# Hybrid decoder trunk on one core: modulation steps behind every second mixing unit, join masks on ScalarE, one form of the 16-block inverses through DRAM

## The chip, the cores and the metric

One Trainium2 chip, one of its cores. The metric is the device time of one execution in microseconds; before the change it is 1177.0 us (median of three runs, 1176.92 to 1178.7). The engines are named as in the profile: PE is TensorE (PEld its weight loads), DVE is VectorE, ACT is ScalarE, POOL is GpSimd, SP the engine that issues most DMAs.

## The reference, cut to what matters

Two layers; in each a half-step SwiGLU FFN, a token-mixing sub-layer and a second FFN, all on 256 tokens of width 1024, each modulated by shift, scale and gate vectors made from `c`. A 64x64 unit-triangular system is inverted for every head and chunk of the mixing's third head group.

```python
def reference(x, c, ...):
    c_act = jax.nn.silu(c)
    for l in range(DEPTH):                                   # 2 layers
        mod = c_act @ w_ada[l] + b_ada[l]                    # 1024 x 9216 matrix: nine vectors
        sh1, sc1, gt1, sh2, sc2, gt2, sh3, sc3, gt3 = jnp.split(mod, N_MOD, axis=-1)
        h = modulate(x, ln_ffn1_g[l], sh1, sc1)
        x = x + 0.5 * gt1[:, None, :] * swiglu(h, ffn1_w_gate[l], ffn1_w_up[l], ffn1_w_down[l])
        h = modulate(x, ln_mix_g[l], sh2, sc2)
        x = x + gt2[:, None, :] * token_mixing(h, w_in[l], ...)
        h = modulate(x, ln_ffn2_g[l], sh3, sc3)
        x = x + 0.5 * gt3[:, None, :] * swiglu(h, ffn2_w_gate[l], ffn2_w_up[l], ffn2_w_down[l])
    return rmsnorm(x, final_g)

def gated_delta_net(q, k, v, g, beta):                       # 6 heads, chunks of 64
    ...
    L = jnp.where(strict, jnp.einsum('bhncd,bhnsd->bhncs', k_beta, k) * decay, 0.0)
    T = lax.linalg.triangular_solve(eye + L, jnp.broadcast_to(eye, L.shape), left_side=True, lower=True)
    u = T @ v_beta
```

## The kernel before

All weights stay in float32 in DRAM and stream through four 1 MB tiles of SBUF (`raw`, N_RAW = 4). A piece of weights is a granule (`gran`); its transfer is issued on SP's queue as soon as the tile that it takes is released. Most granules are then converted into a high and a low part, `hi` by ScalarE and `lo` by VectorE (`convert`), at most six units ahead of their use (N_UNIT), and each product is three matmuls. The units named in WHOLE (`gqk`, `cg`, `ca`, `gv`) are read by PE straight from the raw tile, which is released when PE is done with it.

The nine modulation vectors of a layer are matrix-vector products. A vector needs four modulation steps (`adaunit` in the plan, `ada_step` when it runs): one 1 MB granule of `w_ada`, and two VectorE operations that multiply its rows by a column of `c_act` and add them to an accumulator (`adaacc` or `Lb`). Then `extract` has PE transpose the accumulator in two halves of four transposes into the bank `px`, VectorE reduces each half, and `complete` adds bias and gain. `need_mod` runs all that is still missing at the place where the vector is wanted; `begin_next` wants the next sub-layer's scale and shift (6 and 7 behind the mixing) before the last two output units of the mixing run.

The sequence in which units are converted is written by `plan_ffn` and `plan_mix`. In the mixing, the function `unit` (L344) counts the converted units (six of `mqk`, four of `mv`, three of `gz`) and puts a modulation step behind the second of them and then behind every fourth; what is left in `todo` comes behind the eight units of the output projection. Layer 0 has eight such steps (vectors 6 and 7), layer 1 has four (vector 7).

The order of each engine's queue is written out by hand-made rules at build time: `Clock` keeps a planned time for every engine (`cost`, `note`), PE works through the units, and at `tick` the side tasks of the mixing (generators that `yield` what they wait for) put in their pieces when the planned clock says that their inputs are ready. The engines then run these queues in order. The planned clock counts nothing for the time in which GpSimd issues its DMAs.

The side tasks that matter here: `decays` makes the decay exponents: VectorE spreads `g` over two tiles (`spread`), PE adds them up, and a small matmul gives `cross`. `pairs` forms the matrices L in LD (buffer `xin_LT`) and sends their 32-blocks to DRAM (`scr_l`). `inverse` reads the 16-blocks from there into `Lb`, and GpSimd inverts them by 15 steps of two short operations, a product into `T` and a subtraction from `W`. The inverses are written in both forms (plain and transposed) to `scr_w`, at their places in zeroed 32-blocks, and read back as `Wc`; PE joins them with the off-diagonal blocks `Um` (LD times a mask, GpSimd) to inverses of 32, and then of 64. `values_beta` transposes `v` by PE; `delta_rule` uses inverses and values. `taps` runs the 31-tap convolution on VectorE, or on ScalarE (product, `ctap`) and GpSimd (sum, `cacc`).

Of the kernel before, what the change touches and what calls it, by code (L numbers as in the profile page):

```python
# [10 lines left out]
F32 = mybir.dt.float32  # L11
# [35 lines left out]
CA = dict(b_ada=0, ln_ffn1_g=72, ln_mix_g=96, ln_ffn2_g=104, conv_b=112, conv_ln_g=114, conv_ln_b=116, gdn_norm_g=118)  # L47
CA_PARTS = (slice(0, 80), slice(96, 119))
CB = dict(conv_w=0, gdn_conv_w=62)
K_OFF = dict(ident=0, blk=128, tri=256, rc=512, rs=768, eye=1024, off=1056, negd=1088, negs=1216, gt=1344, winit=1472)  # L50
K_RES = 1088
K_W = 1728


def shape_constants():
    k = np.zeros((128, K_W), np.float32)
    i = np.arange(128)
    o = K_OFF
    k[:, o["ident"]:o["ident"] + 128] = np.eye(128)
    k[:, o["blk"]:o["blk"] + 128] = (i[:, None] // 64 == i[None, :] // 64)  # L60
    k[:, o["gt"]:o["gt"] + 128] = i[:, None] > i[None, :]
    k[:, o["tri"]:o["tri"] + 256] = i[:, None] <= np.arange(256)[None, :]
    k[:, o["negd"]:o["negd"] + 128] = np.where(i[None, :] < i[:, None], -1e30, 0.0)
    k[:, o["negs"]:o["negs"] + 128] = np.where(i[None, :] > i[:, None], -1e30, 0.0)
    half = 8
    inv = np.exp(np.float32(-math.log(500000.0)) * np.arange(0, 16, 2, dtype=np.float32) / np.float32(16))
    ang = np.arange(S, dtype=np.float32)[:, None] * inv.astype(np.float32)[None, :]
    cos, sin = np.cos(ang).T, np.sin(ang).T
    rc, rs = np.ones((64, S), np.float32), np.zeros((64, S), np.float32)
    rc[:half], rc[half:16] = cos, cos  # L70
    rs[:half], rs[half:16] = -sin, sin
    k[:, o["rc"]:o["rc"] + S] = np.concatenate([rc, rc])
    k[:, o["rs"]:o["rs"] + S] = np.concatenate([rs, rs])
    k[:, o["eye"]:o["eye"] + 32] = i[:, None] % 32 == np.arange(32)[None, :]
    k[:, o["off"]:o["off"] + 32] = (i[:, None] % 32 < 16) & (np.arange(32)[None, :] >= 16)
    k[:, o["winit"]:o["winit"] + 256] = np.eye(16, dtype=np.float32).reshape(1, 256)
    return k

# [99 lines left out]
def trunk(ctx, tc, t, out):  # L178
# [31 lines left out]
    prow = {}  # L210
    sp.dma_start(out=kc[:, 0:128], in_=t["konst"][:, 0:128])
    sp.dma_start(out=crow, in_=t["c"].rearrange("a (k p) -> (a k) p", p=128))
    K = {n: kc[:, o:o + {"tri": 256, "rc": 256, "rs": 256, "eye": 32, "off": 32}.get(n, 128)] for n, o in K_OFF.items() if o < K_RES}
    ident = K["ident"]

    def load_rows(l):
# [121 lines left out]
    def plan_mix(l, ada):  # L338
# [5 lines left out]
        def unit(name, i, g, view, width=D):  # L344
# [3 lines left out]
            count[0] += 1  # L348
            if todo and count[0] >= count[1]:
                adaunit(*todo.pop(0))  # L350
                count[1] += 4

        def columns_of(name, c0, n):
            for c in range(0, n, 256):
# [649 lines left out]


    scr_l = nc.dram_tensor("scr_l", [12, 4, 32, 32], F32, kind="Internal").ap()
    scr_w = nc.dram_tensor("scr_w", [2, 12, 4, 32, 32], F32, kind="Internal").ap()
    late = {}

    def mixing(l, G, normed, nxt):  # L1010
# [187 lines left out]
        def decays():  # L1198
# [12 lines left out]

            spread(0)
            spread(1)
            yield from room()
            p = pside([128, NH])
            mm(p, gt.bitcast(F32), g[:, 0], True)
            dve.tensor_tensor(cross, p, lnbeta[:, 0, NH:], op=OP.add)
            for b in range(3):
                R = Rs[b % 2]
                yield (R,)  # L1220
                yield from room(2)
                d = pside([128, 2, 2, 128], True)
                x = pside([128, 2, 128], True)
# [56 lines left out]
            ev["PT"] = True  # L1280

        def values_beta():
            yield from until("v")
            v = ev["v"]
            vb = sb([128, 2, 384], "vb")
            for i in range(2):
# [75 lines left out]
                dve.tensor_tensor(w[:, 0], og[:, b], h[:, 0], op=OP.subtract)  # L1362
            ev["gdn_done"] = True

        W = sb([96, 2, 16, 16], "W")
        sp.dma_start(out=W[:, 0].rearrange("p c i -> p (c i)"), in_=t["konst"][0:96, K_OFF["winit"]:K_OFF["winit"] + 256])
        QUAD = [slice(32 * q, 32 * q + 32) for q in range(4)]

        def put(dst, src, scale=1.0):
# [5 lines left out]
        def inverse():  # L1375
# [8 lines left out]
            for i in range(2):  # L1384
                c = slice(16 * i, 16 * i + 16)
                qd.dma_start(out=Lb[48 * i:48 * i + 48], in_=scr_l.rearrange("h b j i -> (h b) j i")[:, c, c])
            LM = LD.rearrange("p h t x -> p (h t) x")
            yield (Lb, W)
            V = W[:, 0]
            for j in range(15):  # L1390
                n, ni = j + 1, 15 - j
                T = sb([96, 64], "T", bufs=2)
# [2 lines left out]
                                 Lb[:, j:j + 1, n:16].to_broadcast([96, n, ni]), op=OP.mult)  # L1395
                gp.tensor_tensor(V[:, 0:n, n:16], V[:, 0:n, n:16], T, op=OP.subtract)
                yield idle("gp")
            gp.tensor_copy(W[:, 1], V.rearrange("p c i -> p i c"))
            cfg["lo_pool"] = True
            C = sb([128, 2, 12, 32], "Wc")  # L1400
            for f in range(2):
                for i in range(2):
                    c = slice(16 * i, 16 * i + 16)
                    qd.dma_start(out=scr_w[f].rearrange("h b c i -> (h b) c i")[:, c, c], in_=W[48 * i:48 * i + 48, f])
            for q in QUAD:
                gp.tensor_tensor(Um[q], LM[q, :, q], K["off"][q].unsqueeze(1).to_broadcast([32, 12, 32]), op=OP.mult)
            for f in (1, 0):
                qd.dma_start(out=C[:, f], in_=scr_w[f].rearrange("h b c i -> (b c) h i"))
            yield from until("kh")
            wide = sb([128, 1536], "S6a")  # L1410
            TA, X64 = (wide[:, o:o + 768].rearrange("p (m i) -> p m i", i=64) for o in (0, 768))
# [531 lines left out]
    for n, (l, ph) in enumerate(order):  # L1943
# [20 lines left out]
        if n == 0:  # L1964
            zero = sb([128, 384], "E", bufs=3)
            gp.memset(zero, 0.0)
            for f in range(2):
                qd.dma_start(out=scr_w[f].rearrange("h b c i -> (h b c i)").rearrange("(p n) -> p n", n=384), in_=zero)
            dve.tensor_copy(negdb, late["neg"][:, 0])
            dve.tensor_copy(negsb, late["neg"][:, 1])  # L1970
            dve.tensor_copy(gt, late["neg"][:, 2])
# [24 lines left out]
```

## Time and profile before

| what | us |
|---|---|
| time, median of three runs | 1177.0 |
| profiled execution, its own time | 1178.1 |
| span of the profiled execution, first to last instruction | 1176.3 |
| PE busy | 1103.2 |
| DVE busy | 875.1 |
| ACT busy | 597.3 |
| POOL busy | 141.9 |

The page's first part gives the busy time of each engine, its second the span in 40 slices, its fourth the chain of work that ended last, which here is three quarters PE. The kernel is not bound by one engine throughout: in the FFNs PE has no gap, while in the mixings of both layers PE waits several times. The share of busy time is an average over these stages, so the stages are read one by one: the waits of PE within a stretch of time, the busy times of all engines in a stretch, and the instructions in order of time around a wait. Most instructions are recorded through one helper (L171), so that they are told apart by the tiles that they write and read.

### The profile page before, as it was taken

How to read it: one execution, taken by the hardware profiler on the slowest of the kernel's cores; microseconds unless marked ns; L12 is line 12 of the kernel's file. 1: busy time of each engine (PE TensorE's matmuls, PEld its weight loads, DVE VectorE, ACT ScalarE, POOL GpSimd, SP SyncE). 2: the span in 40 equal slices, each digit the busy share in tenths (PEclk: the TensorE clock that was granted, in tenths of full speed). 3: DMA queues.
4: the chain of work that ended last, by engine and by line, in shares of the span. 5: the costliest groups of instructions: out<-in, count | busy, mean ns of one | idle time of the engine just before them, and what ended most of it. 6: DMA issues, size and time to landing. Idle time of an engine off the chain costs nothing.

```text
span 1176.3 us, 22000 instructions
## 1 busy us (share of the span) xinstructions
PE 1103.2 (94%) x9085; PEld 1037.8 (88%) x9085; DVE 875.1 (74%) x1350; ACT 597.3 (51%) x1011; POOL 141.9 (12%) x187
## 2 busy tenths in 40 slices
PE   5799999999969689999999999999996999999997
PEld 4799999968868689999999999997785899999996
DVE  5778778757977788867779887774877869766554
ACT  4364444448356464534456444444764676544443
POOL 0710000020650010000001000001037101000002
PEclk9899999999989999999999999999998999999999
DMA  9759798846423558968864997882562434876640
GB/s 327 251 171 345 282 335 279 265 123 198 125 100 131 186 173 298 329 237 318 287 228 159 333 331 254 306 287 80 166 202 75 145 102 157 310 239 216 208 132 36
DMA packets 167660, 256.52 MB, mean 218 GB/s; under 512 B 8272, under 2 KB 134056, under 8 KB 167560
## 3 DMA queue, kind: packets, MB, share of 16 engines
q1 hardware_dynamic: 166536, 252.95, 63.5%
q0 software_dynamic: 1024, 2.16, 0.8%
q8 instruction: 71, 1.16, 0.4%
q14 instruction: 29, 0.24, 0.1%
HBM read 252.86 MB, written 2.23 MB: 217 GB/s over the span
## 4 chain that ended last, share of the span: by engine, by line
PE 74%; DVE 10%; ACT 7%; POOL 4%; issue 2%; DMA 2%; SPq 0%; POOLq 0%; ACTq 0%; DVEq 0%
PE pm L171 45%; PE pa L171 26%; DVE adaacc L171 3%; PE px L171 2%; DVE lo L171 2%; ACT hi L171 1%; ACT tmp L171 1%; ACT L171 1%; POOL xin_LT L171 1%; DMA raw<-in_w_in_dram 1%; DVE S3a L171 1%; DVE mod L171 1%; POOL W L171 1%; DMA xin_LT<-in_x_dram 1%; DVE v L171 1%
## 5 line engine op out<-in xcount | busy, mean ns | idle before, releaser
L171 PE MATMUL pm<-H,hi 128*128 128x256 f32 x2816 | 510.0, 283 | 1.2 <-DVE H L171 1.2
L171 DVE TENSOR_TENSOR lo<-raw,hi 128x1024 fp32r<-128x1024 f32 (+1 forms) x300 | 361.3, 1227 | 110.9 <-ACT hi L171 110.4
L171 PEld LDWEIGHTS pm<-H,hi 128*128 128x128 f32 x2816 | 433.7, 190 | 4.3 <-DVE H L171 1.4
L171 ACT CAST hi<-raw 128x1024 fp32r<-128x1024 f32 (+1 forms) x306 | 311.5, 1042 | 193.1 <-PE pm L171 84.2
L171 PE MATMUL pm<-H,lo 128*128 128x256 f32 x1408 | 393.0, 281 | 0.0
L171 PEld LDWEIGHTS pm<-H,lo 128*128 128x128 f32 x1408 | 265.4, 189 | 0.0
L171 PE MATMUL pa<-Y,hi 128*128 128x256 f32 x1312 | 236.3, 283 | 3.7 <-DVE xT L171 3.7
L171 PEld LDWEIGHTS pa<-Y,hi 128*128 128x128 f32 x1312 | 202.6, 191 | 4.3 <-DVE xT L171 4.3
L171 PE MATMUL pa<-Y,lo 128*128 128x256 f32 x656 | 184.6, 281 | 0.0
L171 PEld LDWEIGHTS pa<-Y,lo 128*128 128x128 f32 x656 | 126.3, 193 | 0.0
L171 POOL TENSOR_TENSOR xin_LT<-xin_LT 128x256 f32<-128x256 f32 x35 | 27.2, 776 | 645.0 <-ACT xin_LT L171 642.7
L171 ACT CAST Y<-tmp 128x256 fp32r<-128x256 f32 x88 | 35.8, 406 | 120.4 <-DVE tmp L171 120.4
L171 DVE SCALAR_TENSOR_TENSOR adaacc<-raw,c_act,adaacc 128x1024 f32<-128x1024 f32 x70 | 93.9, 1342 | 1.6
L171 DVE SCALAR_TENSOR_TENSOR Lb<-raw,c_act,Lb 128x1024 f32<-128x1024 f32 x56 | 71.8, 1282 | 4.3 <-DMA raw<-in_w_ada_dram 3.0
L171 DVE TENSOR_TENSOR Y<-tmp,Y 128x256 fp32r<-128x256 f32 x88 | 37.4, 425 | 41.6 <-ACT Y L171 41.6
L171 PE MATMUL pm<-Y,raw 128*128 128x256 f32 x288 | 65.9, 382 | 0.0
L171 PEld LDWEIGHTS pm<-Y,raw 128*128 128x128 f32 x288 | 53.6, 190 | 7.5
L171 PE MATMUL pa<-hi,Y 128*128 128x512 f32 x176 | 54.8, 393 | 0.0
L171 ACT ACTIVATE tmp<-pm 128x256 f32<-128x256 f32 x78 | 29.6, 379 | 49.4 <-PE pm L171 49.3
L171 DVE TENSOR_REDUCE mod<-px 128x4 f32<-128x512 f32 x34 | 23.5, 690 | 38.5 <-PE px L171 38.4
L171 DVE SCALAR_TENSOR_TENSOR cacc<-hc,colB,cacc 128x256 f32<-128x256 f32 x92 | 44.7, 499 | 4.6 <-POOL cacc L171 3.1
L171 DVE TENSOR_TENSOR tmp<-tmp,pm 128x256 f32<-128x256 f32 x80 | 33.2, 415 | 12.1 <-ACT tmp L171 12.1
(302 smaller groups left out, 1278.3 us busy)
## 6 DMA issues: line engine op xcount, KB each, us to landing
raw<-in_w_ada_dram SPq DMA_DIRECT2D x70, 1024.0 KB
raw<-in_ffn_w_gate_dram SPq DMA_DIRECT2D x44, 1024.0 KB
raw<-in_ffn_w_up_dram SPq DMA_DIRECT2D x44, 1024.0 KB
raw<-in_ffn_w_down_dram SPq DMA_DIRECT2D x44, 1024.0 KB
raw<-in_w_in_dram SPq DMA_DIRECT2D x12, 1024.0 KB
raw<-in_w_in_dram SPq DMA_DIRECT2D x20, 512.0 KB
raw<-in_w_out_dram SPq DMA_DIRECT2D x16, 512.0 KB
raw<-in_w_in_dram SPq DMA_DIRECT2D x4, 768.0 KB
```

What stands on the lines that cost most here:

```text
L171: return getattr(real, op)(*args, **kw)
```

## The change

Four things are edited. Modulation steps stand behind every second converted unit of the mixing, from the second on, so that the sequence becomes mqk 0 and 1, step, mqk 2 and 3, step, and so on; six of layer 0's eight steps and all four of layer 1's come before the output units. The masking of LD for the join is done by four ScalarE copies with a per-partition scale of 0 or 1 (new constant `half`), with a GpSimd memset of the other half, both before the inverses' steps. The inverses are written in one form only, by two DMAs instead of four, and read by one instead of two; VectorE turns the 32-blocks for the other form; a copy on GpSimd goes. In `decays` the small matmul for `cross` comes behind the wait for the first spread, and `values_beta` waits until the inverses' steps have been issued (`back`).

```diff
-                count[1] += 4
+                count[1] += 2
...
-    scr_w = nc.dram_tensor("scr_w", [2, 12, 4, 32, 32], F32, kind="Internal").ap()
+    scr_w = nc.dram_tensor("scr_w", [12, 4, 32, 32], F32, kind="Internal").ap()
...
             spread(1)
-            yield from room()
-            p = pside([128, NH])
-            mm(p, gt.bitcast(F32), g[:, 0], True)
-            dve.tensor_tensor(cross, p, lnbeta[:, 0, NH:], op=OP.add)
             for b in range(3):
                 R = Rs[b % 2]
                 yield (R,)
+                if b == 0:
+                    yield from room()
+                    p = pside([128, NH])
+                    mm(p, gt.bitcast(F32), g[:, 0], True)
+                    dve.tensor_tensor(cross, p, lnbeta[:, 0, NH:], op=OP.add)
...
         def values_beta():
-            yield from until("v")
+            yield from until("v", "back")
...
                 qd.dma_start(out=Lb[48 * i:48 * i + 48], in_=scr_l.rearrange("h b j i -> (h b) j i")[:, c, c])
+            yield (LD,)
             LM = LD.rearrange("p h t x -> p (h t) x")
+            gp.memset(Um[:, :, 0:16], 0.0)
+            for q in QUAD:
+                act.activation(Um[q, :, 16:32], LM[q, :, q.start + 16:q.stop], AF.Copy, scale=K["half"][q, 0:1])
             yield (Lb, W)
-            V = W[:, 0]
+            V = W
...
-            gp.tensor_copy(W[:, 1], V.rearrange("p c i -> p i c"))
             cfg["lo_pool"] = True
+            ev["back"] = True
             C = sb([128, 2, 12, 32], "Wc")
-            for f in range(2):
-                for i in range(2):
-                    c = slice(16 * i, 16 * i + 16)
-                    qd.dma_start(out=scr_w[f].rearrange("h b c i -> (h b) c i")[:, c, c], in_=W[48 * i:48 * i + 48, f])
-            for q in QUAD:
-                gp.tensor_tensor(Um[q], LM[q, :, q], K["off"][q].unsqueeze(1).to_broadcast([32, 12, 32]), op=OP.mult)
-            for f in (1, 0):
-                qd.dma_start(out=C[:, f], in_=scr_w[f].rearrange("h b c i -> (b c) h i"))
+            for i in range(2):
+                c = slice(16 * i, 16 * i + 16)
+                qd.dma_start(out=scr_w.rearrange("h b c i -> (h b) c i")[:, c, c], in_=V[48 * i:48 * i + 48])
+            qd.dma_start(out=C[:, 0], in_=scr_w.rearrange("h b c i -> (b c) h i"))
+            yield (C[:, 0],)
+            dve.transpose(C[:, 1].rearrange("p m i -> p (m i)"), C[:, 0].rearrange("p m i -> p (m i)"))
```

The rest of the diff follows from these: the constants' offsets move by two columns, the tile `W` and the zeroing of `scr_w` lose the second form.

## Rows read from the trace of the kernel before

**Rows 1.** The page's first part, all engines; share of the span and instructions:
```profile
PE 1103.2 (94%) x9085; PEld 1037.8 (88%) x9085; DVE 875.1 (74%) x1350; ACT 597.3 (51%) x1011; POOL 141.9 (12%) x187
```

**Rows 2.** Waits of PE, 232 to 437 us; us in total, times, longest:
```profile
PE px L171 <- DVE adaacc L171: 8.4, 2, 4.8
PE pa L171 <- DMA Wc<-scr_w: 6.4, 1, 6.4
...
PE pa L171 <- DVE g_g L171: 1.6, 1, 1.6
...
PE pa L171 <- ACT v L171: 1.1, 1, 1.1
```

**Rows 3.** Stretches: length, busy of PE, PEld, DVE, ACT, POOL; clock, DMA share, GB/s:
```profile
258.00:382.40 124.40, 111.39 (x1075) 95.60 (x1074) 99.97 (x219) 75.23 (x163) 39.30 (x62) 0.96 0.45 140
382.40:436.80 54.40, 41.55 (x309) 40.06 (x308) 43.37 (x70) 26.49 (x46) 5.64 (x7) 0.91 0.58 194
828.80:953.20 124.40, 110.78 (x1074) 95.11 (x1073) 99.74 (x218) 74.91 (x162) 38.34 (x62) 0.96 0.46 139
953.20:992.80 39.60, 37.40 (x302) 37.11 (x301) 32.22 (x60) 26.35 (x47) 5.66 (x7) 0.96 0.48 160
```

**Rows 4.** Groups of instructions, DVE, 232 to 436 us; busy, mean ns, idle before:
```profile
L171 DVE SCALAR_TENSOR_TENSOR adaacc<-raw,c_act,adaacc 128x1024 f32<-128x1024 f32 x14 | 18.0, 1284 | 0.4
...
L171 DVE STREAM_SHUFFLE tmp<-Y 128x256 f32<-128x256 f32 x6 | 2.4, 443 | 0.0
```

**Rows 5.** Order of time, PE, end of layer 0's mixing; start, us; idle before:
```profile
398.20 0.66 PE L171 MATMUL px<-kc,adaacc 128*128 128x128 f32 x4 [3.58 <-DVE adaacc L171]
399.64 0.99 PE L171 MATMUL px<-kc,adaacc 128*128 128x128 f32 x4 [0.79 <-DVE mod L171]
...
411.61 1.08 PE L171 MATMUL px<-kc,adaacc 128*128 128x128 f32 x4 [4.81 <-DVE adaacc L171]
```

**Rows 6.** Order of time, PE, end of layer 1's mixing:
```profile
972.96 0.89 PE L171 MATMUL px<-kc,adaacc 128*128 128x128 f32 x4 [2.20 <-DVE mod L171]
```

**Rows 7.** Order of time, SP's queue, first third of layer 0's mixing:
```profile
267.75 0.39 SPq L171 DMA_DIRECT2D raw<-in_w_in_dram  x1
...
272.31 1.02 SPq L171 DMA_DIRECT2D raw<-in_w_in_dram  x2
```

**Rows 8.** Order of time, POOL, the inverses' steps and their way out, layer 0:
```profile
304.92 0.45 POOL L171 TENSOR_TENSOR W<-W,T 96x48 f32<-96x48 f32 x1
...
312.40 0.88 POOL L171 TENSOR_TENSOR W<-W,T 96x48 f32<-96x48 f32 x1
...
316.20 1.07 POOL L171 COPY W<-W 96x256 f32<-96x256 f32 x1
317.22 2.92 POOL L171 DMA_DIRECT2D scr_w<-W  x4
320.15 5.33 POOL L171 TENSOR_TENSOR Lb<-xin_LT,kc 32x384 f32<-32x384 f32 x4
```

**Rows 9.** Order of time, PE, the join of layer 0:
```profile
329.90 1.50 PE L171 MATMUL pa<-Wc,Lb 32*32 32x32 f32 x96 [6.42 <-DMA Wc<-scr_w]
```

**Rows 10.** DMA issues of the whole span; times, KB each, median us to landing:
```profile
Wc<-scr_w POOLq DMA_DIRECT2D x4, 192.0 KB, 4.1
...
scr_l<-xin_LT POOLq DMA_DIRECT2D x8, 48.0 KB, 4.7
scr_w<-W POOLq DMA_DIRECT2D x8, 48.0 KB, 2.8
```

**Rows 11.** Order of time, ACT, 284 to 345 us:
```profile
328.81 0.51 ACT L171 ACTIVATE ctap<-hc,colB 128x256 f32<-128x256 f32 x1 [10.93 <-POOL cacc L171]
...
337.25 1.46 ACT L171 ACTIVATE S6a<-pa 32x384 f32<-32x384 f32 x3 [0.85 <-PE pa L171]
```

**Rows 12.** Order of time, DVE, 284 to 345 us:
```profile
321.73 1.51 DVE L171 TENSOR_TENSOR Y<-Y,kc 128x512 f32<-128x512 f32 x1
...
342.93 0.68 DVE L171 TENSOR_TENSOR Y<-Y,kc 128x512 f32<-128x512 f32 x1
```

## What the change should do to the time

> **What bounds the kernel now.** I read the page first: TensorE (PE) is busy for 94% of the span [rows 1], so the kernel is PE's queue, worked in order, and only what makes PE wait or lowers its clock can be won back. Second, who PE waited for in layer 0 from the first mixing matmul to the next FFN [rows 2]: 8.4 us for the accumulator of the modulation vectors (`adaacc`), 6.4 us for the 16-block inverses coming back from DRAM (`Wc`), 1.6 us for `g_g`, 1.1 us for `v`. The reader is to see that all four belong to waits that the diff touches. Third, the stretches [rows 3]. The middle of the mixing, from 258.0 to 382.4, takes 124.4 us in both layers with about 13 us of PE idle, so layer 1 repeats layer 0 there. The end of the mixing, from the first output matmul to the start of the next FFN's steady loop, takes 54.4 us in layer 0 and 39.6 us in layer 1. The work there is the same form; what differs is that five modulation steps are left over in layer 0 and one in layer 1 (8 and 4 steps, three of them earlier in each). That difference of 14.8 us is the largest thing in sight. It holds idle time and clock: granted 0.91 against 0.96 on average, the low level of the two being 1.2 of 2.4 GHz.
>
> The sum below is made against the profiled execution: 1178.1 us, of which the span is 1176.3 and 1.8 lies around it. It stands 1.1 us over the median of 1177.0, so what the sum gives for that execution is lowered by 1.1 at the end.
>
> **The change part by part.**
> *Steps behind every second unit.* The counter sees the 13 units mqk, mv and gz. Steps came behind units 2, 6, 10; now behind 2, 4, 6, 8, 10, 12. Layer 0 moves three of its five late steps forward (two stay), layer 1 its only one. A step is one 1 MB transfer on SP's queue and two VectorE operations of 1284 ns [rows 4].
> - End of layer 0. Layer 1's end is the model: one step left, 39.6 us. Layer 0 will have two left, one step more, 2 x 1.28 = 2.6 us on VectorE ahead of the transposes for which PE waits: 42.2 instead of 54.4, **-12.2 us**. PE's two waits of 3.58 and 4.81 [rows 5] should become one of about 4 to 5. Bounds: -14.8 if the extra step hides in VectorE's idle time (32.2 busy of 39.6 in layer 1, rows 3); -7.7 if only the six moved operations count (6 x 1.28).
> - End of layer 1. Its wait of 2.20 [rows 6] goes, since the vector is complete earlier; what falls with it is some of the low clock (0.96 of 39.6 is 1.6 us lost): 2.2 + 1.3 = **-3.5**. Bounds -1 and -4.5. Next late there is VectorE's conversion of FFN weights.
> - What the middle pays on VectorE. Six operations in layer 0 (at most 7.7 us), two in layer 1 (2.6), into a stretch where it is busy 100.0 of 124.4 us. It has 24 us to give, and part of its work is freed (below); waits of PE for it there are short now. I take a fifth, **+2.0** in all; bounds 0 and 10.3.
> - Layer 0's first late vector is now complete in the middle, so its 8 transposes on PE (0.66 + 0.99 us, rows 5) go there; the comparison of the ends doesn't hold them: **+1.6**. If they are placed before VectorE has finished, PE waits there: **+1.0**, bounds 0 and 4.8 (the longest such wait at the end, rows 5).
>
> *The ring of raw tiles and SP's queue.* Four tiles rotate; each transfer waits for the release of a tile. The second step's transfer now comes ahead of the weights `ca`, in the slot that SP issues at 267.75; `ca` moves to the slot of 272.31 [rows 7], 4.6 us later. Behind it the `gv` weights wait for that step's operations. This bears on the next part.
>
> *`cross` behind the spread.* The matmul that made PE wait 1.6 us for `g_g` [rows 2] now follows VectorE's first spread; PE does the following unit instead. That unit's successors need `ca` sooner, which comes 4.6 later: of 1.6 I keep **-1.0 a layer**, bounds -1.6 and +3.0 (4.6 less 1.6).
>
> *The inverses' way back.* Now, in layer 0 [rows 8]: GpSimd's chain ends at 316.20; copy 1.07, four writes 2.92 (0.73 each), four masks 5.33, then the reads; PE starts the join at 329.90 after a wait of 6.42 [rows 9], so it came at 323.48. After: two writes at 316.20 and 316.93; a landing of 2.8 (scr_w's own, rows 10) gives 319.7. The read then waits at the head of GpSimd's queue; in front of it stands nothing else, behind it the memset and the taps of the convolution. About 0.5 later it is issued, 320.2, and lands 4.1 later [rows 10]: 324.3. VectorE's turn of 128x384 has no row; the nearest are the 128x256 shuffle, 443 ns [rows 4], as the floor and 1284 ns, a 128x1024 operation, as the ceiling; I take 443 x 1.5 = 0.66, since a shuffle is nearest to it. With 0.5 for signals PE can start at 325.5, **4.4 earlier**. The wait is new on VectorE: behind the turn are queued the decay products and softmax maxima, which wait with it, at most 2 us if it gets there at 322. The Trainium skill ("VectorE: DVE Perf Modes", The three transpose paths) gives 311 ns for 128x128 in bf16; by that the turn is an estimated 0.93 and the sum 0.5 higher over both layers; no row here shows it.
>  The order of PE's queue is written by the planner, whose own chain from the last inverse step to the join also gets about 1.1 shorter (one copy and the masks out, one turn in), so some 1.1 us less work stands in front of the join. With the 1.1 us that PE no longer loses to `v` (`values_beta` waits for `back`), PE comes at 321.3 and waits 4.2 instead of 6.4 + 1.1: **-3.3 a layer**. Bounds: 0 (a landing of 4.7, as scr_l's of the same size, rows 10, and a chain drawn out) and -7.5 (no wait left). The low clock behind the wait stays, as a wait of 3.58 [rows 5] also was followed by slow matmuls.
>
> *Masks and memset, at nothing.* Four ScalarE copies of 32x192, at most 0.49 each (1.46 for three of 32x384, rows 11), early, where ScalarE is busy 75 of 124 us; if uncovered 2 us a layer. GpSimd's memset lies in the wait for the landing of `Lb`. GpSimd gets to the taps some 6 us sooner; ScalarE, held 10.93 by them [rows 11], is released as much sooner, and VectorE behind it. This is why I price the moved steps low. Constants and one zeroing transfer fewer: nothing.
>
> VectorE's 128x512 product took 1.51 beside GpSimd's masks and 0.68 without them [rows 12], and one GpSimd subtraction 0.88 against 0.45 for the same form [rows 8]: two engines hold each other up. The Trainium skill says why ("SBUF — State Buffer", SBUF: two separate sides): VectorE with two SBUF operands and GpSimd share a port pair, and the one that comes second waits out the other's whole instruction; the two rows agree. By that rule the masks' move also frees VectorE, but a step moved beside the inverse chain holds GpSimd: it speaks against this change, and is the second rival.
>
> **Sum.** -12.2 - 3.5 + 2.0 + 1.6 + 1.0 - 2 x 1.0 - 2 x 3.3 = -19.7. The execution 1178.1 becomes 1158.4; less 1.1, **1157.5 us**, faster by 1.7%.
>
> **The rivals.**
> 1. *VectorE becomes the bound of the middle.* The moved operations show in full: 10.3 instead of 2.0, 1157.5 + 8.3 = 1165.8. For it: 80% busy, taps and conversions in one queue. Against: 24 us idle in each middle, and ScalarE's release.
> 2. *The join's wait stays.* A moved step falls beside the inverse chain, whose 30 short operations each can be held for one 1284 ns operation: 2.6 for a step, and a landing of 4.7 instead of 2.8 adds 1.9; 4.5 eats the 4.4 that PE would have started sooner, so 3.3 a layer are lost: 1164.1. The port rule named above gives this. For it: 0.88 against 0.45. Against: by the order of the units the third step falls before the chain and the fourth behind it.
> 3. *More than forecast.* PE has other work for all of the remaining 4.2 a layer, and without the wait the low clock goes too (0.96 of 124.4 is 5 us a layer; half of it): 1157.5 - 8.4 - 5 = 1144. Against: the planner doesn't count GpSimd's issue time, so it will place the join too early again.
> 4. *Slower: the ring starves PE.* Each step between the units takes a tile from the weights; ten of them stand there now (six and four) against six. If each puts off PE by the 4.6 of rows 7: +46, less the 19.7 gained, 1204. It decides from 2 us for each of the ten. Against: the units are converted up to six ahead, and the core's DMA share in the middles is 0.45 [rows 3]. Only the whole units (`ca`, `gv`) are read straight from the ring.
> 5. *It doesn't do what it says:* the planner's waits hold the moved steps back to where they were, and little but the join moves: about 1172.
>
> **How the numbers follow.** Forecast 0.45, first rival 0.18, second 0.17, third 0.12, fourth 0.05, fifth 0.03. Together the first two give 1172.4, still faster. A measurement of this kernel can tell 0.2% (2.4 us) from no change: faster 0.91, within it 0.04 (most of the fifth and the worst of the first two together), slower 0.05. The range is 1146 to 1170: the forecast with its bounds, rivals 1 and 2, and the weak half of rival 3; outside are the rest.
>
> **What would show it.** The stretch from the first output matmul to the next FFN at 42 us in layer 0 and 36 in layer 1; no more than two modulation steps behind the last output conversion in layer 0, none in layer 1. PE's wait at the join about 4, ended by VectorE's turn, the join starting some 9 us after the chain's last subtraction instead of 13.8; no wait for `g_g` or `v`. VectorE in the middle 108 us busy in layer 0, ScalarE's long wait for the taps down to about 5. Wrong would be: PE waiting for `raw` of `ca` or `gv` by more than 1 us, for `adaacc` in the middle by more than 2, a middle that is longer than 124 us, or a join wait of 6 again.

## The result: slower by 0.6%, where 1.7% faster was forecast

| | us |
|---|---|
| before, median of six runs beside it | 1178.3 (1176.9 to 1180.0) |
| changed kernel, median of six runs | 1184.3 (1182.6 to 1190.4) |
| ratio, with its 95% interval | 1.0062 (1.0036 to 1.0087) |
| profiled execution of the changed kernel, its span | 1182.0 |

The forecast was 1157.5, the range 1146 to 1170. The stretches of [rows 3] in the changed kernel, by the same marks (the first matmul of `cg`, the first output matmul, the next FFN; columns as there):

```profile
256.38:393.00 136.62, 116.49 (x1083) 99.34 (x1082) 108.46 (x230) 76.83 (x165) 33.31 (x57) 0.91 0.46 148
393.00:435.42 42.42, 38.07 (x301) 37.26 (x300) 33.91 (x62) 26.42 (x46) 5.64 (x7) 0.92 0.53 174
827.50:960.46 132.96, 112.95 (x1079) 96.43 (x1077) 102.15 (x219) 82.26 (x173) 42.60 (x63) 0.95 0.43 136
960.46:997.94 37.48, 36.90 (x293) 36.37 (x294) 27.46 (x54) 24.58 (x45) 5.63 (x7) 0.95 0.44 141
```

| stretch | before | forecast | measured |
|---|---|---|---|
| layer 0, middle | 124.4 | about 124 | 136.6 |
| layer 0, end | 54.4 | 42.2 | 42.4 |
| layer 1, middle | 124.4 | about 120 | 133.0 |
| layer 1, end | 39.6 | 36.1 | 37.5 |

Both ends came out as forecast; the middles, which were to pay next to nothing, became 12.2 and 8.6 us longer. The busy time of PE says where: in the first middle it is idle for 20.1 us instead of 13.0, and it worked at a mean granted clock of 0.91 instead of 0.96. Who PE waits for, by the view of [rows 2]:

```profile
PE px L172 <- DVE mod L172: 7.6, 2, 5.3
PE pa L172 <- ACT E L172: 6.4, 2, 5.0
PE pm L172 <- DMA raw<-in_w_in_dram: 3.1, 1, 3.1
...
PE px L172 <- DVE adaacc L172: 1.9, 1, 1.9
PE pm L172 <- DVE v L172: 1.7, 1, 1.7
```

All four waits of [rows 2] that the diff was aimed at are gone or short (`Wc`, `g_g` and ScalarE's `v` are gone, `adaacc` went from 8.4 to 1.9). Others took their places: the sum of a vector that is now extracted in the middle (`mod`), the softmax (`E`) and a weight granule (`raw`). Around the join of layer 0, in order of time, POOL's queue first:

```profile
320.56 1.48 POOL L172 DMA_DIRECT2D scr_w<-W  x2 [0.30 <-POOL W L172]
323.94 1.04 POOL L172 DMA_DIRECT2D Wc<-scr_w  x1 [1.91 <-DMA scr_w<-W]
325.01 0.73 POOL L172 TENSOR_TENSOR cacc<-cacc,ctap 128x256 f32<-128x256 f32 x1
```

VectorE:

```profile
325.78 0.48 DVE L172 SCALAR_TENSOR_TENSOR cacc<-hc,colB,cacc 128x256 f32<-128x256 f32 x1 [7.20 <-POOL cacc L172]
...
327.87 2.94 DVE L172 SCALAR_TENSOR_TENSOR adaacc<-raw,c_act,adaacc 128x1024 f32<-128x1024 f32 x2
...
338.05 0.56 DVE L172 STREAM_TRANSPOSE Wc<-Wc 128x384 f32<-128x384 f32 x1
...
342.71 0.68 DVE L172 TENSOR_REDUCE mod<-px 128x4 f32<-128x512 f32 x1
```

PE:

```profile
328.52 1.22 PE L172 MATMUL pa<-Q,S3a 64*128 64x256 f32 x2 [5.02 <-ACT E L172]
...
343.45 1.12 PE L172 MATMUL px<-kc,adaacc 128*128 128x128 f32 x4 [5.34 <-DVE mod L172]
...
347.63 1.02 PE L172 MATMUL pa<-Wc,Lb 32*32 32x32 f32 x96
```

Read the three together. Up to the read the way back did what was forecast: the chain of inverse steps had ended at 320.3, the first of the two writes was started at 320.56, and the read is issued 3.4 us behind that. But behind the read stands a tap of the convolution on GpSimd (325.01); VectorE's next tap needs its sum and waits 7.20 for it, with all that is queued behind: softmax maxima, a modulation step, the rotary steps, and the turn, which runs at 338.05, 14.1 us after the read was issued. PE joins another 9.6 later, since the second half of the extraction (343.45) stands in front of the join and waits for VectorE too.

### The profile page after: what moved, and what is told of

It reads as the page before. It is cut to its first block, busy times and chain, and to the rows that moved or that the text cites. A ratio compares the mean times of both kernels' runs of the same rounds, so it can differ in the third digit from the quotient of the medians.

```text
span 1182.0 us, 22029 instructions
## 1 busy us (share of the span) xinstructions
PE 1103.2 (93%) x9085; PEld 1036.2 (88%) x9085; DVE 872.6 (74%) x1348; ACT 604.5 (51%) x1024; POOL 139.5 (12%) x182
## 4 chain that ended last, share of the span: by engine, by line
PE 74%; DVE 12%; POOL 4%; DMA 4%; ACT 3%; issue 2%; SPq 0%; POOLq 0%; DVEq 0%; ACTq 0%
PE pm L172 44%; PE pa L172 28%; DVE lo L172 3%; DVE adaacc L172 3%; PE px L172 2%; DMA raw<-in_w_in_dram 2%; POOL xin_LT L172 1%; DVE tmp L172 1%; POOL W L172 1%; POOL T L172 1%; DVE mod L172 1%; DVE S3a L172 1%; DMA scr_l<-xin_LT 1%; DMA Lb<-scr_l 1%; DMA xin_LT<-in_x_dram 1%
## 5 line engine op out<-in xcount | busy, mean ns | idle before, releaser
L172 POOL TENSOR_TENSOR cacc<-cacc,ctap 128x256 f32<-128x256 f32 x38 | 39.0, 1031 | 160.2 <-ACT ctap L172 128.7
L172 ACT ACTIVATE tmp<-pm 128x256 f32<-128x256 f32 x78 | 29.6, 379 | 48.1 <-PE pm L172 48.1
L172 DVE SCALAR_TENSOR_TENSOR cacc<-hc,colB,cacc 128x256 f32<-128x256 f32 x82 | 36.0, 481 | 20.3 <-POOL cacc L172 19.9
L172 DVE TENSOR_REDUCE mod<-px 128x4 f32<-128x512 f32 x34 | 23.4, 689 | 35.3 <-PE px L172 35.3
```

The source lines that it names most:

```text
L172: return getattr(real, op)(*args, **kw)
```

## The experiments

The theories, as the expectations letter them: A, the moved steps lengthen the middles; B, GpSimd's queue behind the landing does; C, the late matmul for `cross`; D, taps of the convolution put on GpSimd behind the inverses; E, a full VectorE; F, the extraction's wait; G, the delta rule and what follows it set the end; H, the turn ties the join to VectorE.

Times below are ratios to runs of the kernel before on the same chip, with their 95% intervals. For reading the traces I used marks of one chain, in us from the first `cg` matmul of the layer: L sent to DRAM (`scr_l`), the inverses read back (`Wc`), the join on PE, the first product of the delta rule, ScalarE's silu of the output gate, and the sum of squares for the next FFN, which closes the mixing. The silu waits for the delta rule's end only where the planner has the delta rule's products behind it by then; in all_but_steps, cross_back and cross_back_taps_late it runs ahead of that end, and its mark can't be set beside the others. Layer 0, and the closing mark of layer 1:

| kernel | ratio | L sent | read | join | delta rule | silu | close | close, layer 1 |
|---|---|---|---|---|---|---|---|---|
| before | 1 | 30.1 | 66.9 | 71.4 | 103.4 | 125.8 | 170.4 | 156.0 |
| changed | 1.0062 | 38.4 | 67.0 | 90.7 | 117.3 | 138.1 | 170.6 | 162.4 |
| steps_alone | 0.994 | 30.2 | 63.0 | 72.5 | 105.2 | 127.5 | 161.6 | 155.7 |
| inverses_alone | 1.0158 | 30.1 | 58.1 | 79.1 | 114.1 | 136.7 | 181.5 | 165.6 |
| cross_alone | 1.022 | 44.5 | 82.4 | 88.3 | 119.6 | 139.4 | 184.2 | 169.8 |
| all_but_steps | 1.0126 | 44.6 | 83.5 | 91.7 | 120.6 | 128.9 | 180.8 | 162.7 |
| inverses_taps_late | 1.0011 | 30.1 | 61.4 | 68.2 | 103.5 | 126.6 | 172.8 | 157.9 |
| masks_back | 1.0062 | 30.1 | 65.1 | 76.6 | 105.3 | 128.8 | 175.0 | 158.8 |
| cross_back | 1.0062 | 30.2 | 60.5 | 85.9 | 121.8 | 133.9 | 171.3 | 166.1 |
| taps_late | 0.995 | 36.9 | 65.4 | 75.2 | 113.1 | 138.0 | 167.9 | 152.1 |
| cross_back_taps_late | 0.9891 | 30.2 | 60.5 | 79.9 | 113.9 | 128.0 | 166.3 | 149.1 |
| two_banks | 0.9885 | 30.2 | 60.5 | 72.3 | 104.7 | 129.3 | 162.4 | 150.2 |
| steps_taps_late | 0.9869 | 30.2 | 62.4 | 75.9 | 104.8 | 129.4 | 161.9 | 152.8 |
| steps_all | 0.9905 | 30.2 | 65.9 | 71.2 | 111.2 | 136.3 | 162.0 | 150.8 |

A mark that holds in every run is VectorE's last conversion of the gated values (`Y<-v,Y`). In layer 0 the close follows it after 36.6 to 40.1 us where five modulation steps are left, after 23.4 to 24.6 where two are, and after 16.6 in steps_all, where none is. Before and changed, VectorE and PE in turn:

```profile
392.31 0.42 DVE L171 TENSOR_TENSOR Y<-v,Y 128x256 fp32r<-128x256 f32 x1 [0.47 <-ACT Y L171]
428.91 0.70 PE L171 MATMUL px<-xin_LT,ones 128*128 128x256 f32 x2 [0.23 <-POOL xin_LT L171]
```

```profile
402.98 0.43 DVE L172 TENSOR_TENSOR Y<-v,Y 128x256 fp32r<-128x256 f32 x1 [0.47 <-ACT Y L172]
427.53 0.70 PE L172 MATMUL px<-xin_LT,ones 128*128 128x256 f32 x2 [0.23 <-POOL xin_LT L172]
```

### The parts one by one

**steps_alone**: before, with `count[1] += 4` made `+= 2`.

> The kernel before with one edit: modulation steps behind every second mixing unit. The forecast's terms for the steps (-12.2, -3.5, +2.0, +1.6, +1.0) give -11.1 us, a ratio near 0.991, and middles that are some 3 us longer in layer 0 and under 2 in layer 1. Theory A (the steps are what lengthens the middles: they stand ahead of the products for L on VectorE and ahead of ca and gv on SP's queue) expects the end of layer 0 shorter by 12 but the middles longer by about 10 and 7: ratio 1.00 to 1.005. Theory B (GpSimd's queue, with the read of the inverses at its head, holds taps, VectorE and ScalarE) expects the same as the forecast here, since the way back is the old one.

Measured 1169.9, 0.994 (0.992 to 0.996). The ends fell by 10.9 and 2.7, the middles grew by 2.1 and 2.4. In sum the forecast's terms for the steps are met (middles 4.5 against 4.6, ends 13.6 against 15.7), and theory A falls. By layers they are not: layer 0 gains 8.8 us, layer 1 0.2, since its middle pays what its end saves. What had no term is PE's wait for a weight granule, which the ring delivers later, in each layer:

```profile
PE pm L171 <- DMA raw<-in_w_in_dram: 2.8, 1, 2.8
```

**all_but_steps**: the changed kernel with `count[1] += 4`.

> The changed kernel with the steps behind every fourth unit as before. The forecast's terms (twice -1.0 and twice -3.3) give -8.6 us, ratio 0.993. Theory A (steps are guilty) expects the same, with PE's join some 4 us earlier than before in each layer. Theory B (GpSimd's queue behind the landing of the inverses) expects middles longer by 6 to 9 us a layer, ratio 1.010 to 1.015, with VectorE and ScalarE waiting some 7 us for cacc behind the read. Theory C (the late cross matmul holds the decays) expects middles longer by 3 to 4 us a layer, ratio near 1.004.

Measured 1193.0, 1.0126 (1.0113 to 1.0139). The loss is not the steps'; they earn 7 us within the change too. L is sent 14 us late, which points at `cross`.

**inverses_alone**: before, with masks on ScalarE, one form through DRAM, and the turn.

> The kernel before with the masks on ScalarE and one form of the inverses through DRAM, turned by VectorE; the steps, the matmul for cross and the values stay as before. The forecast's term gives -6.6 us, ratio 0.994, as do theories A (steps) and C (cross). Theory B (GpSimd's queue) expects ratio 1.01 or more. Beside all_but_steps it shows what cross and the values' wait are worth.

Measured 1196.7, 1.0158 (1.0145 to 1.0171). POOL, VectorE and PE, in order of time:

```profile
315.08 1.05 POOL L172 DMA_DIRECT2D Wc<-scr_w  x1 [1.91 <-DMA scr_w<-W]
316.15 0.73 POOL L172 TENSOR_TENSOR cacc<-cacc,ctap 128x256 f32<-128x256 f32 x1
```

```profile
300.61 0.48 DVE L172 SCALAR_TENSOR_TENSOR cacc<-hc,colB,cacc 128x256 f32<-128x256 f32 x1
316.92 0.48 DVE L172 SCALAR_TENSOR_TENSOR cacc<-hc,colB,cacc 128x256 f32<-128x256 f32 x1 [15.82 <-POOL cacc L172]
```

```profile
321.18 0.80 PE L172 MATMUL pa<-Y 64*128 64x128 f32 x4 [9.64 <-DVE Y L172]
```

The read is issued 8.8 us earlier than before, and the join comes 7.7 later. A tap between two of VectorE's was given to GpSimd, whose queue gets to it at 316.15, behind the chain, the writes and the read; VectorE stands still for 15.82, and the rotary steps behind its tap make PE wait 9.64. Theory B (GpSimd's queue) had the direction, but it is the tap, not the read's wait for its landing (1.91).

**cross_alone**: before, with the small matmul behind the first wait for R.

```diff
-            yield from room()
-            p = pside([128, NH])
-            mm(p, gt.bitcast(F32), g[:, 0], True)
-            dve.tensor_tensor(cross, p, lnbeta[:, 0, NH:], op=OP.add)
             for b in range(3):
...
                 yield (R,)
+                if b == 0:
+                    yield from room()
+                    p = pside([128, NH])
+                    mm(p, gt.bitcast(F32), g[:, 0], True)
+                    dve.tensor_tensor(cross, p, lnbeta[:, 0, NH:], op=OP.add)
```

> The kernel before with the matmul for cross behind the wait for the first spread, and nothing else. The forecast's term: -2.0 us, ratio 0.998. Theory C (cross then stands behind conversions on VectorE, and the decays, L and the inverses come later by that) expects the wait of 1.6 for g_g gone but L's last product 3 us later and the time the same or up to 4 us longer, ratio 1.000 to 1.004.

Measured 1203.8, 1.022 (1.0202 to 1.0239): 26 us, where I had put -2 and theory C at most +4. VectorE:

```profile
273.75 2.35 DVE L171 TENSOR_TENSOR lo<-raw,hi 128x1024 fp32r<-128x1024 f32 x2
...
276.62 0.16 DVE L171 TENSOR_TENSOR g_c<-pa,g_x 128x6 f32<-128x6 f32 x1
...
299.24 1.14 DVE L171 TENSOR_TENSOR xin_LT<-pa,PT 128x256 f32<-128x256 f32 x4
```

and POOL:

```profile
298.47 3.89 POOL L171 TENSOR_TENSOR cacc<-cacc,ctap 128x256 f32<-128x256 f32 x5 [0.89 <-ACT ctap L171]
302.30 2.49 POOL L171 DMA_DIRECT2D scr_l<-xin_LT  x4
```

VectorE in before, and ScalarE in cross_alone:

```profile
270.15 0.16 DVE L171 TENSOR_TENSOR g_c<-pa,g_x 128x6 f32<-128x6 f32 x1
```

```profile
276.87 0.37 ACT L171 ACTIVATE PT<-pa,g_c 128x128 f32<-128x128 f32 x1 [2.30 <-DVE g_c L171]
```

An addition of 0.16 us now stands behind two conversions. Counted from the first `cg` matmul it comes 7.2 us later than in before, the first of ScalarE's exponentials that need it 3.5 later; each following piece slips a place in some queue, L is complete 12.6 us later and sent 14 us later, and the delta rule starts 16 us later.

**cross_taps_late**: cross_alone with `cfg["lo_pool"] = False` ahead of the first spread.

> cross_alone with no tap on GpSimd ahead of L's way to DRAM. In cross_alone six taps of GpSimd, 0.77 and 3.89 us and the gaps between them, stood ahead of that transfer: it was issued at 302.30, L's last product having ended at 300.4. Theory C alone (L itself is late by 12) expects little: 2 us a layer at most, ratio 1.018 or more. If the taps are half of it, the ratio is near 1.01.

Measured 1202.8, 1.0207 (1.0185 to 1.0228): the taps ahead of L's transfer are not it. L is late by itself.

### The two causes, one undone at a time

**cross_back**: the changed kernel with cross_alone's diff reversed.

> The changed kernel with the matmul for cross ahead of the first spread again, as before. Theory C (cross is the head of the chain decays, L, inverses, join, which ends last in the middle; cross_alone cost 26 us) expects L's last product by 288 and the join 10 us or more earlier than in the changed kernel, with a time of 1170 or less, ratio 0.993 or less. Theory D (a tap of the convolution put on GpSimd behind the inverses holds VectorE's next tap and all that is queued behind it; inverses_alone showed 15.8) expects that most of the 19 us of inverses_alone remain: ratio 1.005 to 1.01. The sum of the single runs (-7.8 for the steps, +19 for the inverses) is 1.0095.

Measured 1186.7, 1.0062 (1.0049 to 1.0074): the same as the changed kernel, as D had it and not C. L is sent 8 us earlier, but the delta rule starts 4.5 us later. VectorE's wait for `cacc` is only 2.4 here; taps can hold it in another way, as its row beside six of GpSimd's taps shows, and the same product in cross_back_taps_late:

```profile
323.97 7.02 POOL L172 TENSOR_TENSOR cacc<-cacc,ctap 128x256 f32<-128x256 f32 x6
328.04 1.22 DVE L172 TENSOR_TENSOR Y<-Y,kc 128x512 f32<-128x512 f32 x1
```

```profile
324.14 0.69 DVE L172 TENSOR_TENSOR Y<-Y,kc 128x512 f32<-128x512 f32 x1
```

It takes 0.69 in cross_back_taps_late, where GpSimd is idle. [rows 12] had shown the same with the masks; the taps took the masks' place. The Trainium skill ("SBUF — State Buffer", SBUF: two separate sides) says that a VectorE instruction with two inputs in SBUF and a GpSimd instruction that reads SBUF share a port pair, and that the one that comes second waits; the two times agree with it.

**inverses_taps_late**, and the same move on cross_back (**cross_back_taps_late**) and on the changed kernel (**taps_late**):

```diff
-            cfg["lo_pool"] = True
             ev["back"] = True
...
             yield (Um, C)
+            cfg["lo_pool"] = True
```

> inverses_alone with one line moved: taps may go to GpSimd again only from the start of the join, not from the last inverse step. Theory D expects VectorE's 15.8 us of waiting for cacc and PE's 9.6 for the rotated queries (Y) gone in both layers: 1196.7 less 2 x 9.6 or more, 1170 to 1178, ratio 0.993 to 1.000. Rival E (VectorE itself is too full there: the turn, the rotary steps and the taps that GpSimd no longer takes) expects that the rotary steps stay late and the ratio at 1.01 or more.

> The changed kernel with both: cross ahead of the spread, and no tap on GpSimd between the last inverse step and the start of the join. If C and D are the two causes and the rest of the forecast held, this is the forecast less its term for cross: 1157.5 plus 2, some 1160, ratio 0.984. Rival E expects 1170 or more. If steps and inverses hinder each other in a third way, it lies above steps_alone (0.994).

> The changed kernel whole, with the taps kept off GpSimd until the start of the join and nothing else. It stands against cross_back_taps_late (0.9891, 13 us faster than before) and shows what the moved matmul for cross costs once the other cause is away. Theory C (cross heads the chain that ends last) expects 10 us or more of loss, ratio 0.998 or above, with L's last product some 4 us later than in cross_back_taps_late. If cross costs nothing here, the ratio is 0.989, as the forecast (0.983) would nearly have it.

Measured 1181.3, 1.0011 (1.0002 to 1.002); 1165.6, 0.9891 (0.9874 to 0.9908); and 1171.0, 0.995 (0.9925 to 0.9976). Theory D holds and rival E falls: one line about taps is worth 17 us on inverses_alone, 13 on the changed kernel, 20 on cross_back. With it, `cross` costs 7 us (0.995 against 0.9891). The causes don't add: `cross` cost 26 alone, 7 here and nothing in the changed kernel.

**masks_back**: inverses_alone with the masks on GpSimd again, behind the writes.

```diff
-            yield (LD,)
...
-            gp.memset(Um[:, :, 0:16], 0.0)
-            for q in QUAD:
-                act.activation(Um[q, :, 16:32], LM[q, :, q.start + 16:q.stop], AF.Copy, scale=K["half"][q, 0:1])
...
+            for q in QUAD:
+                gp.tensor_tensor(Um[q], LM[q, :, q], K["off"][q].unsqueeze(1).to_broadcast([32, 12, 32]), op=OP.mult)
             qd.dma_start(out=C[:, 0], in_=scr_w.rearrange("h b c i -> (b c) h i"))
```

> inverses_alone with the four masks on GpSimd again, behind the writes of the inverses as before; taps are free to go to GpSimd from the last inverse step on. Theory D in its full form says that the masks' 5.7 us in the planned time of GpSimd had kept taps off its queue; with them back, some 14 taps on GpSimd instead of 22, VectorE's wait for cacc under 3 us instead of 15.8, ratio 0.995 to 1.003. If the masks are not what kept the taps off, the ratio stays at 1.016.

Measured 1184.5, 1.0062 (1.0042 to 1.0083), between the two. GpSimd's taps in layer 0 of before, inverses_alone and masks_back, in this order:

```profile
L171 POOL TENSOR_TENSOR cacc<-cacc,ctap 128x256 f32<-128x256 f32 x14 | 12.4, 891 | 23.3 <-DVE cacc L171 15.6 <-ACT ctap L171 7.1
```

```profile
L172 POOL TENSOR_TENSOR cacc<-cacc,ctap 128x256 f32<-128x256 f32 x22 | 19.8, 901 | 43.4 <-ACT ctap L172 32.3 <-DVE cacc L172 8.7 <-DVE sm L172 2.0
```

```profile
L172 POOL TENSOR_TENSOR cacc<-cacc,ctap 128x256 f32<-128x256 f32 x19 | 16.5, 875 | 26.8 <-DVE cacc L172 15.7 <-ACT ctap L172 8.7 <-ACT E L172 1.8
```

VectorE's longest wait for `cacc` fell from 15.8 to 0.9. So the masks kept some taps away, three of the eight that had come, and the right ones: `taps` gives one to ScalarE and GpSimd when VectorE's planned time is more than 2 us ahead of PE's and theirs is not, and by `cost` the masks and the copy are 6.7 us of that time (four of 1.42 and one of 0.98). The planner doesn't see that GpSimd gets there later in truth. What brought the other five isn't shown. The rest of D's numbers missed: 19 taps and not 14, and PE waits 7.8 for the turn, which runs 10.8 us after the read's issue. It stands behind the rotary steps, and these behind a conversion that waits for ScalarE; ScalarE in turn waits for GpSimd's first tap, behind masks and read. ScalarE and VectorE:

```profile
324.15 0.51 ACT L172 ACTIVATE ctap<-hc,colB 128x256 f32<-128x256 f32 x1 [12.54 <-POOL cacc L172]
```

```profile
326.29 1.05 DVE L172 TENSOR_TENSOR lo<-raw,hi 128x768 fp32r<-128x768 f32 x1 [8.11 <-ACT hi L172]
333.07 0.56 DVE L172 STREAM_TRANSPOSE Wc<-Wc 128x384 f32<-128x384 f32 x1
```

**old_taps_late** (before with the late taps, the control) and **steps_taps_late** (steps_alone with them):

> The kernel before with the taps kept off GpSimd until the start of the join, and nothing else: the control for steps_taps_late (0.9869) and inverses_taps_late (1.0011). If the late taps are a gain of their own, 0.993; if they only mend what steps or inverses bring with them, 1.000.

> steps_alone with the taps kept off GpSimd until the start of the join, and with the old way back of the inverses. It tells what the inverses' new way is worth beside the steps: cross_back_taps_late had 0.9891. If the new way brings the 3 us a layer that inverses_taps_late showed in both middles (-3.7 and -3.5), this run lies at 0.994 like steps_alone; if what cross_back_taps_late won is the late taps themselves, it lies at 0.989 too.

Measured 0.9997 (0.9988 to 1.0006) and 1164.1, 0.9869 (0.9851 to 0.9887). Late taps are no gain on the old kernel; but they shorten its middles by 2.4 and 3.6 us, which the ends give back. And the steps with the old way back of the inverses are as fast as the best with the new way (0.9891, 0.9885): the new way is worth nothing. steps_taps_late, 14.6 us faster than before, is the fastest kernel of the study, beside steps_banks below, which is no different.

### What sets the end of the mixing

**two_banks**, **steps_banks**: cross_back_taps_late and steps_taps_late with the halves of the extraction in two PSUM banks.

```diff
-        p = ps([128, 4, 128], cfg["wide"][h])
+        p = bank((128, 4, 128)) if h and cfg.get("mid") else ps([128, 4, 128], cfg["wide"][h])
...
         hparts = hh, hl = htile(0), htile(1)
+        cfg["mid"] = True
...
         state["out"] = True
+        cfg["mid"] = False
```

> cross_back_taps_late with the two halves of the modulation vector that is extracted in layer 0's middle in two PSUM banks, so that the second half of the transposes need not wait for VectorE's sum of the first (PE waited 5.23 for it). Theory F (that wait is what is left of layer 0's loss) expects 5 us less and more with the clock, ratio 0.985 or below. If PE only waits for the next thing instead, the ratio stays at 0.989.

> steps_taps_late with the two halves of the extraction in layer 0's middle in two PSUM banks. In steps_taps_late PE did not wait for the sum of the first half, since the halves stand apart in its queue; so theory G (the end of the mixing is set by the delta rule and what follows it on ScalarE and VectorE, not by PE's waits in the middle) expects no change, 0.987, and a PE-bound middle would give 0.985.

Measured 0.9885 (0.9862 to 0.9907) and 0.9869 (0.9855 to 0.9883): no change that the intervals can tell. In two_banks the join of layer 0 comes 7.6 earlier and the first output matmul 10, but the mixing closes only 3.9 earlier. Theory F falls. For G, the silu's mark says nothing here (128.0 and 129.3), since it runs ahead of the delta rule's end in the one and behind it in the other. ScalarE's silu and VectorE's last step of the delta rule, cross_back_taps_late first:

```profile
384.89 0.84 ACT L172 ACTIVATE Q<-Q 128x768 f32<-128x768 f32 x1
394.99 0.42 DVE L172 TENSOR_TENSOR v<-v,tmp 128x256 f32<-128x256 f32 x1 [1.07 <-ACT tmp L172]
```

```profile
386.55 0.85 ACT L172 ACTIVATE Q<-Q 128x768 f32<-128x768 f32 x1
385.27 0.43 DVE L172 TENSOR_TENSOR v<-v,tmp 128x256 f32<-128x256 f32 x1 [0.25 <-ACT tmp L172]
```

The delta rule ends 10 earlier, but with the silu now behind it the last conversion comes only 2.8 earlier (139.0 against 141.8), and the close follows that: what G says of the end holds.

**steps_all**: steps_banks with layer 0's eight steps behind units 2, 3, 5, 6, 8, 9, 11 and 12.

```diff
-                count[1] += 2
+                count[1] += 1 + (len(todo) + len(ada) // 8) % 2 if len(ada) == 8 else 2
```

> steps_banks with all eight steps of layer 0 between the mixing units (behind units 2, 3, 5, 6, 8, 9, 11, 12). From the activation of the output gate to the next FFN the stretch took 44.6 us with five steps left and 32.5 with two; layer 1 takes 24.8 with none. Theory G expects about 25 in layer 0 as well, 7.5 less, if the delta rule is not later by it: ratio 0.981. If the two more steps hold up VectorE or the ring of raw tiles in the middle, that is eaten and the ratio is 0.987 or worse.

Measured 1166.8, 0.9905 (0.9884 to 0.9926). From the silu to the close it took 25.7, as G said (44.6 in before, 33.1 in steps_banks). But the delta rule starts 9 us later than in steps_banks (102.3), and PE waits for the ring:

```profile
297.15 3.18 PE L171 MATMUL pm<-Y,raw 128*128 128x256 f32 x7 [8.92 <-DMA raw<-in_w_in_dram]
```

The wait is of the fourth rival's kind, with two steps more than the change moves. That it delays the delta rule isn't shown: it lies ahead of the join, and the join is not later for it (71.2 against 72.1); the 9 us arise behind the join.

**values_free** (cross_back_taps_late without `back`) and **two_forms** (steps_taps_late with the masks on ScalarE, both forms still through DRAM):

> cross_back_taps_late (0.9891) without the wait of the transposed values for the end of the inverses' steps; it isolates the last part of the change. The forecast had put it at nothing but the 1.1 us that PE waits for v: 0.989 to 0.990.

> steps_taps_late with the masks on ScalarE and GpSimd's memset ahead of the inverses' steps, but both forms of the inverses still written and read, so that VectorE has nothing to turn. Theory H (the turn ties the join to VectorE's queue: it ran 14.1 us after the read was issued in the changed kernel, 3.7 to 17.5 in the others, where the landing alone takes 4) expects the join at 70 to 71 us from the first cg matmul instead of 72 to 80, and a time of 0.987 or better. If the turn costs nothing, it lies at cross_back_taps_late's 0.989, and if one form less through DRAM was the gain, above that.

Measured 0.9887 (0.987 to 0.9904): `back` costs nothing. And 1166.3, 0.9899 (0.9881 to 0.9917): theory H falls. With no turn the join of layer 1 comes at 73.6, exactly where it was with it, and that of layer 0 at 81.7, behind the extraction's wait of 5.16. The turn is late where VectorE has been held up by taps, and elsewhere PE's own order sets the join.

## Why the prediction was wrong

- **End of layer 0, -12.2:** right, -12.0, and by its own reasoning: two steps left instead of five. The wait there, predicted as one of 4 to 5, came as two, of 1.9 and 2.2. Layer 1's -3.5 was -2.1.
- **VectorE's load and the extraction in the middle, +4.6:** the sum is met for the steps by themselves (4.5 in steps_alone), but by luck: nearly all of it was forecast for layer 0, and it came as 2.1 and 2.4, with a wait of 2.8 for the ring in each layer that had no term. Beside the rest of the change the forced wait of the second half was 5.34, above the bound of 4.8.
- **The ring:** priced at nothing but a later `ca`; it costs a wait of 3.1 in layer 0 and 3.0 in layer 1. My mark for "wrong" was 1 us.
- **`cross`, -1.0 a layer, bounds -1.6 and +3.0:** wrong in sign and far out of bounds. The step that failed is the one that looked at PE's wait of 1.6 alone and called the delay 4.6 of `ca` the worst. What matters of that matmul is who reads its result: the exponentials, hence L, hence the inverses; and the delay grew along that chain, from 3.5 at the first exponential that needs it to 12.6 at L and 16 at the delta rule (cross_alone).
- **The way back, -3.3 a layer:** its working was right up to the read (forecast 4.0 behind the chain's end, it was 3.7). The middles of inverses_taps_late (-3.7 and -3.5) look like the rest of it, but old_taps_late has nearly the same (-2.4 and -3.6) with the old way back: they are the late taps' doing for the most part. Two steps failed. First, "GpSimd gets to the taps some 6 us sooner; ScalarE is released as much sooner, and VectorE behind it": the order of the queues is written from planned times, and taking 6.7 planned us off GpSimd brought it more taps (22 for 14 in inverses_alone, 16 in the changed kernel), put in front of VectorE's work. I treated the queues' order as fixed where the change feeds the rule that writes it. Second, the turn was costed by its length (0.66; it took 0.56) and by what waits behind it, not by what stands ahead of it in VectorE's queue: 14.1 us from read to turn. This second one follows from the first; a turn alone costs nothing measurable (two_forms).
- **The measure itself:** the sum added PE's waits as if each were time. In inverses_taps_late 3.7 us less middle gave a mixing that closes 2.4 later, in two_banks 10 less gave 3.9. What closes the mixing of layer 0 is the chain L, inverses, delta rule, silu, last conversions, remaining steps. The changed kernel took 12.1 off its last link (last conversion to close 36.6 to 24.5) and delayed its start by as much (133.8 to 146.1): layer 0 is 0.2 longer. Layer 1 is 6.4 longer, and that is the whole loss. Its last conversion comes 6.6 later, and the step saved behind it brings nothing: where no step is left, 15.5 to 16.8 us from conversion to close are enough in the other runs, but here it is 21.7, because PE begins its output matmuls 8.6 us later than before and needs 29.6 for them up to the close.
- **The rivals:** none had this. The second named the draw-out of the chain and the shared ports, and with its 1164.1 was still on the wrong side; the fourth's price per step was 0.6 (6.1 us for ten steps), not the 2 from which it decides. The 0.05 for slower was too low, because all four parts were priced one by one on a kernel whose order is made anew with each of them. (The forecast's last line has a slip as well: 1158.4 less 1.1 is 1157.3, not 1157.5; nothing hangs on it.)

What stays open: why the late `cross` costs nothing in the changed kernel as it stands (1.0062 with it and without), and 7 us once the taps are kept away. And where VectorE's wait for `cacc` is short (cross_back), the runs show that GpSimd's taps cost 20 us, but not how much of that is the order of the queues and how much the slower operations beside them.

## What to carry to other kernels

Before an operation is moved or freed, follow its result to the chain that closes the stage, and price the delay there; a wait of PE that is not on that chain can be removed for nothing, and a 0.16 us addition on it can cost 13 us a layer. Where a planner writes the queues, work taken off an engine is an invitation to put other work there: list which rule reads that engine's planned time, and what in-order partner then waits. Try the parts of a change singly: here one of four earned 0.6% (1.3% with a line that keeps the taps away), and two of the others ate it.

## What the runs showed of the hardware

- VectorE's turn of 128x384 in float32 took 0.56 to 0.58 us, under my estimate of 0.66. The estimate from the Trainium skill's page ("VectorE: DVE Perf Modes", The three transpose paths) was 0.93; the measurement decides.
- Beside GpSimd's taps a 128x512 product of VectorE took 1.22 us, where 0.69 was its time beside an idle GpSimd. The taps took 0.88 to 1.02 us on average over layer 0, and 0.72 to 0.75 at the least.
- In these runs a DMA issue at the head of GpSimd's queue that waited for a landing (1.91 us) held the taps behind it, and VectorE, which adds to the same accumulator in turns with GpSimd, stood still until the whole queue ahead was done, 15.82 us at worst.
